# A hand-written order of all instructions, searched anew, in a 3x3 convolution with 2x2 max pooling

## Chip, cores and metric

One core of a Trainium2 chip runs the program. The metric is the device time of one execution in microseconds (us), the median of several runs.

## The reference

A 3x3 convolution with zero padding of one row and column, 16 images of 64 channels and 64x64 pixels, 128 output channels, and then the maximum over 2x2 squares:

```
x: (16, 64, 64, 64) float32, weight: (128, 64, 3, 3) float32, pool_size 2
x_pad = pad(x, 1)
conv[b, co, i, j] = sum over ci, kh, kw of weight[co, ci, kh, kw] * x_pad[b, ci, i + kh, j + kw]
output[b, c, i, j] = max(conv[b, c, 2i:2i+2, 2j:2j+2])          # (16, 128, 32, 32) float32
```

## The kernel before

Two images lie on the 128 partitions, 64 channels each, so a matmul uses one half of the rows of TensorE (PE) and two of them, one for each image, run side by side. A pair of images is cut into four chunks of 8 output rows; there are 32 chunks, numbered 0 to 31 in the order of their work. Eight are of the kind K (0, 2, 5, 9, 14, 18, 23, 27), the others of the kind W. A and B are the even and the odd convolution rows of a chunk. Rows are combined before the matmuls, so that A and B share products: a W chunk `s` and image `l` go through these steps, each named by a token.

- `LX.s` loads the rows into one of four buffers `wx` (SP's queue); `LK.s` loads a K chunk with a cast to bf16 (POOL's queue).
- `E.s`, `S.s` and `V.s` are sums and differences of rows (L195, or L289 where `CP.s`, an ACT copy of rows to PSUM, L285, gave one of the operands). `KS.s` is the sum of a K chunk. Tokens end in the engine: `v` is DVE, `a` is ACT, `g` is POOL. A row operation on POOL is made to wait for the last one on DVE ahead of it in the order (`row_op`, L194 to L199).
- `P2.s.l` starts A with `E`; `SE.s.l` copies it to B's PSUM bank (ACT, L422); `P0` and `P3` add `V` to A and to B; `EV` takes A to SBUF (ACT, L409 or L411); `MX` puts the maximum of A and B into B's bank (DVE, L426); `P1` adds `S`, which both have in common; `OD` copies the odd columns out (ACT, L449), `CM` takes the maximum with the even ones (DVE, L458), and `ST` stores the chunk.
- A K chunk has `PAa`, `PAb` for A, `PBa`, `PBb` for B and `PR` in place of `P1`; it reads its rows as they are, after `XE` and `XO` have cast them (even and odd rows) where they came as float32.

All products go through L394. Each has three matmuls of up to 512 columns, and two products that stand next to each other in the order, one for each image, are emitted alternately (`flush`). A number at the end of a product or of `SE` is its PSUM bank, one of eight; a bank is free again when its last reader is done.

The weights come in by `LW`. Seven combinations are made: `c.D2` and `c.D0` (differences of the kernel's rows, L205 and L207), `c.g0` to `c.g2` (casts), and `c.GS`, `c.GM`, `c.GP` (sums; GM and GP need GS). `T.x` transposes a combination on PE (L228), `TV.x` copies it back to SBUF (L239, L241, L243). `PAa` uses D2, `PAb` and `P0` G0, `PBa` D0, `PBb` and `P3` G2, `P2` GM, `PR` G1 and `P1` GP.

The order of everything is written out in one string, `ORDER`: a token is emitted when its turn comes, so each engine gets its own instructions in the order of the string, and semaphores follow from the data. Some loads also wait for the end of an earlier chunk (`paced`).

```
for token in ORDER.split():
    what, _, at = token.partition(":")
    name, *args = what.split(".")
    ...
```

Of the kernel before, what the change touches and what calls it, by code (L numbers as in the profile page):

```python
# [27 lines left out]
SE.6.1:5 MX.4.1 PR.2.0 PR.2.1 E.7:v P0.6.1 P1.4.0 SE.6.0:3 LX.12 OD.2.0 OD.2.1 EV.6.1 P3.6.1 P0.6.0
OD.4.0 EV.6.0 CM.2.0 P3.6.0 P1.4.1 CM.2.1 MX.6.1 CM.4.0 OD.4.1 PAa.5.1:6 P2.7.0:1 MX.6.0 CP.8:4
LX.15 PAa.9.0:0 P1.6.1 OD.6.1 CM.4.1 LX.16 CM.6.1 SE.7.0:2 P1.6.0 PAb.5.1 P2.7.1:7 PAb.9.0 ST.0  # L30
S.7:g PAa.9.1:5 P0.7.0 V.8:g E.8:v OD.6.0 E.10:g EV.5.1 EV.9.0 S.8:v CM.6.0 EV.7.0 KS.9:v PBa.5.1:6
P3.7.0 LK.14 PAb.9.1 PAa.5.0:4 ST.2 KS.5:v SE.7.1:0 CP.11:3 PBb.5.1 P2.8.0:1 V.10:g MX.7.0 E.11:v
LX.13 PAb.5.0 P0.7.1 MX.5.1 EV.9.1 P1.7.0 P3.7.1 S.11:v SE.8.0:5 E.12:v EV.7.1 P0.8.0 PR.5.1 EV.5.0
P2.10.1:7 PBa.5.0:3 OD.7.0 S.10:g MX.7.1 P2.8.1:4 P3.8.0 OD.5.1 CM.5.1 ST.4 V.12:g EV.8.0 P1.7.1
PBb.5.0 CM.7.0 SE.10.1:1 P0.10.1 P2.10.0:6 MX.8.0 MX.5.0 SE.8.1:2 OD.7.1 EV.10.1 CM.7.1 SE.10.0:0
P1.8.0 P3.10.1 ST.6 P0.8.1 PR.5.0 OD.8.0 P3.8.1 P2.12.0:7 MX.10.1 OD.5.0 P0.10.0 P1.10.1 CM.8.0
CM.5.0 EV.8.1 SE.12.0:5 P3.10.0 P2.11.1:4 MX.8.1 ST.1 LX.19 EV.10.0 P0.12.0 P1.8.1 SE.11.1:3 P3.12.0
PBa.9.1:6 V.11:g OD.8.1 OD.10.1 EV.12.0 LX.17 MX.10.0 LK.18 P1.10.0 P0.11.1 OD.10.0 S.12:v CM.8.1
CM.10.1 PBb.9.1 PAa.14.0:2 MX.12.0 EV.11.1 CM.10.0 P2.11.0:7 P3.11.1 ST.5 ST.3 CP.13:1 PAb.14.0
PAa.14.1:4 MX.9.1 SE.11.0:0 MX.11.1 EV.14.0 E.13:v P1.12.0 PR.9.1 OD.12.0 S.13:v P0.11.0 P1.11.1  # L40
OD.9.1 OD.11.1 CM.12.0 P2.13.1:2 P3.11.0 CM.11.1 EV.11.0 CM.9.1 MX.11.0 CP.17:5 SE.13.1:3 PBa.9.0:1
PAb.14.1 V.13:g PBb.9.0 P2.12.1:7 LX.22 S.16:g EV.14.1 E.16:g E.17:v SE.12.1:6 P1.11.0 P0.13.1
OD.11.0 EV.13.1 V.16:g P2.13.0:4 P3.13.1 MX.9.0 P0.12.1 PR.9.0 S.17:v SE.13.0:5 MX.13.1 P2.16.0:2
P3.12.1 EV.12.1 CM.11.0 E.15:g MX.12.1 OD.9.0 SE.16.0:7 P0.13.0 P1.13.1 OD.13.1 CM.9.0 LX.20 P3.13.0
P2.15.1:0 EV.13.0 V.15:g CM.13.1 MX.13.0 SE.15.1:1 P0.16.0 P1.12.1 ST.11 P2.15.0:3 PBa.14.1:4
KS.18:v P0.15.1 P3.16.0 ST.8 S.15:v KS.14:v OD.12.1 P1.13.0 PBb.14.1 CM.12.1 EV.16.0 SE.15.0:2
EV.15.1 P0.15.0 P3.15.1 LX.24 MX.14.1 PBa.14.0:6 P2.16.1:0 ST.10 MX.15.1 LX.21 P3.15.0 PR.14.1
EV.15.0 OD.13.0 SE.16.1:3 MX.16.0 PBb.14.0 P1.15.1 OD.14.1 CM.13.0 P2.17.1:5 P1.16.0 OD.15.1 LK.23
OD.16.0 MX.15.0 V.17:g CM.14.1 CM.15.1 P0.16.1 P1.15.0 SE.17.1:4 EV.16.1 P3.16.1 P2.17.0:1 MX.14.0
CM.16.0 V.20:g OD.15.0 MX.16.1 PR.14.0 P0.17.1 S.19:g SE.17.0:7 P3.17.1 PAa.18.0:0 CM.15.0 OD.14.0  # L50
P1.16.1 P0.17.0 CM.14.0 EV.17.1 CP.22:2 E.19:g MX.17.1 PAb.18.0 PAa.18.1:6 E.22:v OD.16.1 EV.17.0
P1.17.1 PBa.18.0:5 EV.18.0 CM.16.1 OD.17.1 S.22:v PAb.18.1 P2.19.0:1 CP.20:3 EV.18.1 CM.17.1
SE.19.0:2 PBa.18.1:0 P3.17.0 P2.19.1:4 PBb.18.0 V.19:g SE.19.1:6 PBb.18.1 P0.19.0 E.20:v S.20:v ST.7
MX.18.0 V.22:g P3.19.0 P0.19.1 MX.18.1 PR.18.0 P2.22.1:3 E.21:g EV.19.0 LX.26 MX.19.0 EV.19.1
PR.18.1 P2.20.0:1 OD.18.0 LX.28 MX.17.0 CM.18.0 V.21:g LX.25 SE.22.1:4 OD.18.1 CM.18.1 P3.19.1
P1.19.0 SE.20.0:5 P1.17.0 P0.22.1 OD.19.0 MX.19.1 P3.22.1 P2.21.0:0 EV.22.1 OD.17.0 CM.19.0 MX.22.1
P0.20.0 P1.19.1 P2.20.1:3 P3.20.0 SE.21.0:2 ST.9 OD.19.1 ST.13 KS.23:v CM.19.1 E.24:g EV.20.0
MX.20.0 P0.21.0 P1.22.1 P3.21.0 P2.21.1:1 LK.27 SE.20.1:6 P0.20.1 P1.20.0 CM.17.0 OD.22.1 CM.22.1
S.21:v EV.21.0 SE.21.1:7 EV.20.1 OD.20.0 V.24:g P3.20.1 P2.22.0:4 V.25:g E.26:g S.24:g MX.21.0
V.28:g P2.24.0:0 P0.21.1 SE.22.0:3 EV.21.1 MX.20.1 P1.21.0 P3.21.1 CM.20.0 OD.21.0 ST.18 SE.24.0:5  # L60
P0.22.0 P1.20.1 MX.21.1 P3.22.0 P2.24.1:1 EV.22.0 P1.21.1 P0.24.0 CM.21.0 LX.30 OD.20.1 SE.24.1:2
P3.24.0 PAa.23.1:4 ST.16 CM.20.1 EV.24.0 PAa.23.0:6 P0.24.1 MX.22.0 OD.21.1 P1.22.0 PAb.23.1 CM.21.1
CP.25:0 EV.24.1 E.25:v MX.24.0 PAb.23.0 PBa.23.1:7 EV.23.1 S.25:v OD.22.0 P2.25.0:1 P3.24.1 MX.24.1
EV.23.0 PBb.23.1 PBa.23.0:4 P2.25.1:6 P1.24.0 LX.29 ST.12 P1.24.1 PBb.23.0 SE.25.0:0 CM.22.0 OD.24.0
SE.25.1:3 MX.23.1 CM.24.0 MX.23.0 KS.27:v P0.25.0 PR.23.1 OD.24.1 EV.25.0 OD.23.1 P3.25.0 P0.25.1
PR.23.0 PAa.27.1:5 CM.24.1 V.26:g MX.25.0 EV.25.1 P2.26.1:1 PAa.27.0:2 ST.14 OD.23.0 ST.19 PAb.27.1
P1.25.0 CM.23.1 PAb.27.0 P3.25.1 CP.30:6 SE.26.1:7 CM.23.0 E.30:v S.30:v PBa.27.0:4 P3.26.1
P2.26.0:6 P0.26.1 EV.27.1 ST.20 OD.25.0 CP.28:5 MX.25.1 EV.27.0 E.28:v CM.25.0 PBb.27.0 P1.25.1
S.28:v S.26:g SE.26.0:2 MX.27.0 EV.26.1 ST.15 E.29:g PBa.27.1:0 P0.26.0 V.30:g MX.26.1 OD.25.1
P3.26.0 P2.28.1:1 EV.26.0 MX.26.0 PBb.27.1 PR.27.0 P1.26.1 P2.28.0:5 CM.25.1 SE.28.1:6 OD.27.0  # L70
V.29:g CM.27.0 ST.24 S.29:g MX.27.1 SE.28.0:3 OD.26.1 P1.26.0 P0.28.1 EV.28.1 P3.28.1 P2.29.0:4
P0.28.0 PR.27.1 OD.26.0 CM.26.1 SE.29.0:1 P2.29.1:7 P3.28.0 OD.27.1 EV.28.0 LX.31 ST.17 MX.28.1
P0.29.0 P1.28.1 CM.26.0 SE.29.1:2 ST.26 OD.28.1 MX.28.0 P3.29.0 P2.30.1:5 EV.29.0 CM.27.1 MX.29.0
SE.30.1:0 E.31:g P0.29.1 P1.28.0 EV.29.1 OD.28.0 P3.29.1 P2.30.0:4 CM.28.1 P1.29.0 P0.30.1 CM.28.0
SE.30.0:7 ST.27 EV.30.1 OD.29.0 MX.29.1 P3.30.1 P2.31.0:6 MX.30.1 ST.23 CM.29.0 ST.28 ST.22 V.31:g
# [509 lines left out]
```

## Time and profile before

| | |
|---|---|
| median of 3 runs | 105.04 us (104.89 to 105.57) |
| the profiled execution | 105.11 us |
| its span, first to last instruction | 103.3 us |
| granted clock of PE, mean | 0.987 |
| busy: PE, DVE, ACT, POOL | 96.6, 90.2, 88.8, 80.6 us |
| bytes moved by DMA | 24.07 MB, mean 233 GB/s |

The profile is of one execution. Busy times of the engines lie beside each other, so their sum says nothing; what counts is which of them is late at a given moment. PE is counted busy while any of its two halves has a matmul under way.

### The profile page before, as it was taken

Reading aid. Unit: us, or ns where it says so; the run is one execution under the profiler, and the core shown is the slowest. Engines: PE = TensorE matmul, PEld = TensorE weight load, DVE = VectorE, ACT = ScalarE, POOL = GpSimd, SP = SyncE. Lnnn points to the kernel's source line nnn. Section 1 sums busy time; section 2 is a strip of 40 time slices with the busy share of each in tenths; the row PEclk is TensorE's granted clock in tenths of the full one; section 3 lists DMA queues with packets and bytes.
Section 4 is the critical chain, followed back from the end, with each engine's and each line's share of the span. In section 5 each row is a group of like instructions: output and inputs, shape, how many; then the busy total and the mean of one; then the engine's idle time right before and its main releaser. Section 6 shows DMA issues by size and latency. Waiting matters only on the chain.

```text
span 103.3 us, 2470 instructions
## 1 busy us (share of the span) xinstructions
PE 96.6 (94%) x869; PEld 51.6 (50%) x869; DVE 90.2 (87%) x179; ACT 88.8 (86%) x198; POOL 80.6 (78%) x61
## 2 busy tenths in 40 slices
PE   6988699999999999999999999999999999999940
...
GB/s 65 260 251 414 420 421 352 303 115 179 36 274 247 215 360 290 309 253 185 205 115 246 309 195 177 360 307 275 186 356 205 142 231 40 0 133 285 337 187 83
DMA packets 13789, 24.07 MB, mean 233 GB/s; under 512 B 1104, under 2 KB 9680, under 8 KB 13776
## 3 DMA queue, kind: packets, MB, share of 16 engines
...
q0 software_dynamic: 864, 1.56, 10.1%
q8 instruction: 7, 0.11, 0.4%
q10 hardware_dynamic: 144, 0.07, 0.2%
...
## 4 chain that ended last, share of the span: by engine, by line
PE 80%; DMA 7%; DVE 4%; ACT 3%; SPq 1%; issue 1%; DVEq 0%
PE acc L394 80%; DMA wx<-in_x_dram 7%; ACT ev L409 1%; DVE o L458 1%; DVE acc L426 1%; ACT acc L422 1%; SPq L266 1%; ACT od L449 1%; DVE wv L195 1%; DVE we L195 0%; SPq L519 0%; DVEq L580 0%; DVE o L468 0%; DVEq L426 0%
## 5 line engine op out<-in xcount | busy, mean ns | idle before, releaser
L394 PEld LDWEIGHTS <-wt 64*128 64x128 bf16 x840 | 49.3, 94 | 42.8 <-issue 3.0
L195 POOL TENSOR_TENSOR wv<-wx 128x1024 bf16<-128x1024 f32 x23 | 54.1, 2363 | 12.9 <-DVE wv L195 9.3
L394 PE MATMUL acc<-wv,wt 64*128 64x504 bf16 (+1 forms) x288 | 61.1, 377 | 0.9 <-DVE acc L426 0.9
L426 DVE TENSOR_TENSOR acc<-acc,ev 128x512 f32<-128x512 f32 x64 | 43.4, 694 | 3.0 <-ACT ev L409 1.3
L394 PE MATMUL acc<-kx,wt 64*128 64x504 bf16 (+6 forms) x216 | 38.2, 350 | 0.2 <-DVE kx L190 0.2
L394 PE MATMUL acc<-we,wt 64*128 64x512 bf16 (+1 forms) x144 | 37.4, 377 | 0.3 <-DVE we L195 0.3
L394 PE MATMUL acc<-ws,wt 64*128 64x512 bf16 x144 | 37.5, 376 | 0.2 <-DVE acc L426 0.2
L409 ACT ACTIVATE ev<-acc 128x512 f32<-128x512 f32 x48 | 29.6, 616 | 1.8 <-PE acc L394 1.3
L422 ACT COPY acc<-acc 128x512 f32<-128x512 f32 x48 | 28.2, 593 | 1.2 <-PE acc L394 0.3
L458 DVE TENSOR_TENSOR o<-acc,od 128x256 f32<-128x256 f32 x63 | 25.4, 418 | 1.9 <-ACT od L449 1.6
L449 ACT COPY od<-acc 128x256 f32<-128x256 f32 x63 | 23.6, 383 | 2.8 <-PE acc L394 2.5
L195 POOL TENSOR_TENSOR ws<-wx 128x512 bf16<-128x512 f32 x9 | 11.5, 1273 | 1.4 <-DVE we L195 1.4
L394 PE MATMUL acc<-ks,wt 64*128 64x504 bf16 (+1 forms) x48 | 11.9, 376 | 0.0
L195 POOL TENSOR_TENSOR we<-wx 128x512 bf16<-128x512 f32 x9 | 11.5, 1275 | 0.4 <-DVE ks L195 0.4
L411 ACT COPY ev<-acc 128x512 f32<-128x512 f32 x16 | 9.4, 599 | 1.2 <-PE acc L394 1.2
L289 DVE TENSOR_TENSOR we<-acc,wx 128x512 bf16<-128x512 f32 x11 | 7.5, 686 | 0.2
L289 DVE TENSOR_TENSOR ws<-acc,wx 128x512 bf16<-128x512 f32 x11 | 7.5, 682 | 0.0
L285 ACT COPY acc<-wx 128x512 f32<-128x512 f32 x11 | 6.7, 610 | 0.8 <-DMA wx<-in_x_dram 0.8
L486 PE MATMUL acc<-const-bfloat16-1.0 128*128 128x512 bf16 x8 | 3.6, 628 | 0.8 <-PEq L566 0.8
L270 POOL DMA_DIRECT2D kx<-in_x_dram x6 | 3.5, 592 | 0.0
L195 DVE TENSOR_TENSOR ks<-kx 128x512 bf16<-128x512 bf16 x8 | 3.4, 438 | 0.0
L195 DVE TENSOR_TENSOR we<-wx 128x512 bf16<-128x512 f32 x4 | 2.7, 684 | 0.7 <-DMA wx<-in_x_dram 0.7
...
## 6 DMA issues: line engine op xcount, KB each, us to landing
...
```

The source lines that it names most:

```text
L195: inst = eng[e].tensor_tensor(out=out, in0=in0, in1=in1, op=op)
L270: paced(s, nc.gpsimd.dma_start(out=kx_of(p)[:, lo:hi, :], in_=rows_of(p, lo, hi)))
L285: nc.scalar.copy(out=acc[bank], in_=wrow(s, 0))
L289: nc.vector.tensor_tensor(out=t, in0=lifted[s], in1=wrow(s, 1), op=op)
L394: yield lambda kw=kw, o0=o0, o1=o1, c0=c0, c1=c1: nc.tensor.matmul(acc[t][:, i0:i1, o0:o1], wt[l * CI : l * CI + CI, K * BLOCKS[block] + T ...
L409: inst = nc.scalar.mul(t, acc[bank["A", s, l]], -1.0)
L411: inst = nc.scalar.copy(out=t, in_=acc[bank["A", s, l]])
L422: nc.scalar.copy(out=acc[b], in_=acc[bank["A", s, l]])
L426: nc.vector.tensor_tensor(out=t, in0=t, in1=ev[s, l], op=MAX)
L449: nc.scalar.copy(out=od[s, l][:, i0:i1], in_=acc[bank["B", s, l]][:, i0:i1, 1::2])
L458: done[s, l] = nc.vector.tensor_tensor(out=outs(s)[:, l, i0:i1], in0=acc[bank["B", s, l]][:, i0:i1, 0::2], in1=od[s, l][:, i0:i1], op=MAX,)
L486: nc.tensor.matmul(acc[n], ones[:, 0:128], ones, start=True, stop=True, skip_group_check=True)
```

## The change

Only `ORDER` is another; the helpers, the tiles and the number of buffers are the same. Both strings hold the same 287 products and transposes and the same 62 issues on SP's queue. These tokens change engine:

| token | before | after |
|---|---|---|
| c.g1 | ACT | DVE |
| c.GS | DVE | POOL |
| TV.D0, TV.G0 | ACT | DVE |
| TV.G2, TV.GM | DVE | ACT |
| XE.0b, XO.0b | DVE | ACT |
| V.4 | POOL | DVE |
| E.4, E.7 | DVE | POOL |
| E.10, E.16 | POOL | DVE |
| S.12, S.21 | DVE | POOL |

Banks and places change throughout. The diff, cut to the head, the places that the text speaks of, and the end:

```
-LW LX.0a c.g0:a LX.0b c.g1:a c.g2:a XE.0a:a c.D0:v T.D0:0 LX.1 XO.0a:a c.D2:v LX.3 T.D2:1 T.G0:2
-LX.2 c.GS:v c.GM:v T.G2:3 T.G1:4 TV.D2:v TV.D0:a XE.0b:v T.GM:5 TV.G0:a LX.4 XO.0b:v PAa.0.0a:6
-PAa.0.1a:7 PBa.0.0a:1 PBa.0.1a:0 TV.G2:v PAa.0.1b PAb.0.0a c.GP:v TV.G1:a TV.GM:v KS.0:v E.1:v
-PAa.0.0b PAb.0.1a PAb.0.1b PAb.0.0b PBa.0.0b PBa.0.1b EV.0.1 EV.0.0 LX.7 PBb.0.1a PBb.0.0a T.GP:2
-TV.GP:a PBb.0.1b PBb.0.0b P2.1.0:3 P2.1.1:4 CP.3:5 V.1:v LX.6 MX.0.1 SE.1.0:7 P0.1.0 PR.0.1 SE.1.1:6
-V.3:g MX.0.0 P0.1.1 PR.0.0 XO.2:a E.3:v EV.1.0 LK.5 OD.0.1 S.3:v EV.1.1 S.1:v PAa.2.0:2 P3.1.1
-XE.2:a CM.0.1 S.4:g MX.1.1 P2.3.0:3 PAa.2.1:5 OD.0.0 P2.3.1:4 PAb.2.0 CM.0.0 KS.2:v E.4:v LK.9 V.4:g
-SE.3.0:0 P1.1.1 P3.1.0 EV.2.0 MX.1.0 SE.3.1:1 OD.1.1 CP.6:2 PAb.2.1 P3.3.0 P0.3.1 P0.3.0 V.6:g LX.11
...
+LW c.D2:v c.D0:v T.D2:0 c.g0:a LX.0a XO.0a:a XE.0a:a LX.0b c.g2:a c.g1:v LX.1 LX.3 TV.D2:v T.D0:1
+T.G0:2 TV.D0:v PAa.0.0a:3 PAa.0.1a:4 LX.2 T.G2:5 PBa.0.0a:6 PBa.0.1a:7 XE.0b:a T.G1:0 c.GS:g TV.G0:v
+XO.0b:a LX.4 TV.G1:a c.GM:v T.GM:1 PAb.0.1a PBa.0.0b LX.7 LX.6 c.GP:v T.GP:2 KS.0:v TV.G2:a PAb.0.0a
+PAa.0.1b PBb.0.0a E.1:v PAa.0.0b PAb.0.1b PBb.0.0b PBb.0.1a TV.GM:a PBa.0.1b PAb.0.0b PBb.0.1b
+EV.0.1 TV.GP:a V.1:v EV.0.0 MX.0.1 P2.1.0:0 P2.1.1:5 CP.3:1 SE.1.0:4 PR.0.1 P0.1.0 E.3:v SE.1.1:3
+XO.2:a EV.1.0 P2.3.1:2 P3.1.0 S.3:v P0.1.1 PAa.2.0:1 V.3:g MX.0.0 S.1:v V.4:v SE.3.1:0 XE.2:a EV.1.1
+LK.5 PR.0.0 P0.3.1 OD.0.0 LX.10 LX.8 OD.0.1 MX.1.0 LK.9 S.4:g E.4:g P3.3.1 PAb.2.0 E.7:g CM.0.0
+EV.3.1 EV.2.0 P2.3.0:5 P3.1.1 MX.1.1 SE.3.0:2 PAa.2.1:6 P1.1.0 V.6:g CM.0.1 OD.1.0 MX.3.1 P1.1.1
+P0.3.0 CP.6:1 CM.1.0 PBa.2.0:7 PAb.2.1 OD.1.1 EV.3.0 E.6:v EV.2.1 P2.4.1:4 P3.3.0 P1.3.1 P2.4.0:5
...
+P2.6.0:0 OD.3.0 KS.2:v P0.4.0 P3.4.1 EV.4.1 V.7:g CM.3.0 SE.6.0:2 MX.2.1 LX.11 MX.4.1 P2.6.1:4
+P3.4.0 EV.4.0 PR.2.1 P0.6.0 SE.6.1:5 MX.4.0 EV.6.0 E.10:v LK.14 P1.4.1 PR.2.0 LX.12 P3.6.0 P0.6.1
...
+OD.4.0 V.10:g SE.7.0:1 CM.2.0 CM.4.0 PAa.5.0:4 PBa.5.1:7 P2.7.1:3 P0.7.0 KS.5:v EV.5.1 S.7:g OD.6.0
...
+LX.13 SE.10.1:4 EV.9.1 SE.10.0:2 P1.8.0 P0.10.1 PBb.5.0 P3.10.1 KS.9:v KS.14:v SE.8.1:5 P0.10.0
+P0.8.1 EV.10.1 E.12:v OD.8.0 S.12:g EV.10.0 P2.11.1:6 P3.10.0 MX.5.0 P3.8.1 PR.5.0 CM.8.0 MX.10.1
+MX.10.0 P2.12.0:3 P1.10.1 EV.8.1 SE.11.1:0 V.12:g LX.16 OD.5.0 P0.11.1 P1.10.0 CM.5.0 OD.10.1 MX.8.1
+SE.12.0:7 EV.11.1 PAa.14.0:1 P3.11.1 ST.2 OD.10.0 E.16:v ST.1 P0.12.0 P1.8.1 OD.8.1 EV.12.0 MX.11.1
...
+CM.13.1 EV.13.0 LX.20 CP.17:1 MX.13.0 P1.12.1 P0.16.0 EV.16.0 E.17:v ST.7 PBa.14.1:5 P3.16.0
+SE.15.1:2 ST.6 S.17:v OD.12.1 CM.12.1 PBb.14.1 P2.15.0:6 SE.15.0:1 ST.11 ST.10 P1.13.0 P0.15.1
...
+PBa.18.1:3 CM.15.0 MX.17.1 PBa.18.0:1 PAb.18.1 E.19:g EV.17.0 ST.8 CM.16.1 CP.22:2 LX.25 P2.19.0:4
...
-P2.31.1:3 P0.30.0 SE.31.0:5 EV.30.0 S.31:g P3.30.0 P1.29.1 MX.30.0 SE.31.1:1 P0.31.0 P1.30.1 OD.29.1
-CM.29.1 EV.31.0 OD.30.1 P3.31.0 P0.31.1 EV.31.1 P1.30.0 P3.31.1 MX.31.0 P1.31.0 OD.30.0 MX.31.1
-CM.30.1 P1.31.1 ST.25 ST.21 ST.29 OD.31.0 ST.30.1 CM.30.0 ST.30.0 CM.31.0 ST.31.0 RM.31.1a RM.31.1b
-ST.31.1a ST.31.1b:a
+MX.30.1 SE.31.0:2 P2.31.1:5 P0.30.0 EV.30.0 P3.30.0 P1.29.1 CM.29.0 MX.30.0 SE.31.1:4 OD.29.1
+P0.31.0 P1.30.1 CM.29.1 ST.28 EV.31.0 P3.31.0 P0.31.1 EV.31.1 MX.31.0 S.31:g P1.30.0 P3.31.1 P1.31.0
+ST.24 MX.31.1 ST.29 OD.30.0 CM.30.0 OD.30.1 CM.30.1 ST.30.0 OD.31.0 ST.30.1 CM.31.0 P1.31.1 ST.31.0
+RM.31.1a RM.31.1b ST.31.1a ST.31.1b:a
```

More of the change, by code (lines that the diff above doesn't have):

```diff
@@ L22 @@
-V.3:g MX.0.0 P0.1.1 PR.0.0 XO.2:a E.3:v EV.1.0 LK.5 OD.0.1 S.3:v EV.1.1 S.1:v PAa.2.0:2 P3.1.1
-XE.2:a CM.0.1 S.4:g MX.1.1 P2.3.0:3 PAa.2.1:5 OD.0.0 P2.3.1:4 PAb.2.0 CM.0.0 KS.2:v E.4:v LK.9 V.4:g
-SE.3.0:0 P1.1.1 P3.1.0 EV.2.0 MX.1.0 SE.3.1:1 OD.1.1 CP.6:2 PAb.2.1 P3.3.0 P0.3.1 P0.3.0 V.6:g LX.11
-CM.1.1 P3.3.1 P1.1.0 E.6:v EV.3.1 EV.2.1 PBa.2.0:6 PBa.2.1:4 EV.3.0 MX.3.1 P2.4.0:5 P1.3.1 OD.1.0
-OD.3.1 S.6:v LX.10 PBb.2.0 P2.4.1:3 MX.3.0 PBb.2.1 P1.3.0 CM.1.0 SE.4.0:2 SE.4.1:7 CM.3.1 OD.3.0
-MX.2.0 V.7:g P2.6.1:1 P0.4.0 CM.3.0 P0.4.1 P3.4.0 EV.4.0 MX.2.1 LX.8 MX.4.0 EV.4.1 P2.6.0:0 P3.4.1
@@ L28 @@
[L28 to L75, printed above, removed]
@@ new lines @@
+P0.3.0 CP.6:1 CM.1.0 PBa.2.0:7 PAb.2.1 OD.1.1 EV.3.0 E.6:v EV.2.1 P2.4.1:4 P3.3.0 P1.3.1 P2.4.0:5
+S.6:v MX.3.0 CM.1.1 SE.4.1:6 OD.3.1 PBb.2.0 PBa.2.1:1 CM.3.1 SE.4.0:3 P1.3.0 P0.4.1 MX.2.0 PBb.2.1
+P2.6.0:0 OD.3.0 KS.2:v P0.4.0 P3.4.1 EV.4.1 V.7:g CM.3.0 SE.6.0:2 MX.2.1 LX.11 MX.4.1 P2.6.1:4
+P3.4.0 EV.4.0 PR.2.1 P0.6.0 SE.6.1:5 MX.4.0 EV.6.0 E.10:v LK.14 P1.4.1 PR.2.0 LX.12 P3.6.0 P0.6.1
+PAa.5.1:0 P1.4.0 OD.4.1 CM.4.1 OD.2.1 EV.6.1 MX.6.0 P3.6.1 P2.7.0:6 PAb.5.1 P1.6.0 CM.2.1 OD.2.0
+OD.4.0 V.10:g SE.7.0:1 CM.2.0 CM.4.0 PAa.5.0:4 PBa.5.1:7 P2.7.1:3 P0.7.0 KS.5:v EV.5.1 S.7:g OD.6.0
@@ new lines @@
+V.8:g MX.6.1 ST.0 PBb.5.1 PAb.5.0 CM.6.0 CP.8:0 EV.7.0 S.10:g V.11:g ST.3 P3.7.0 P1.6.1 SE.7.1:2
+E.8:v MX.5.1 S.8:v P0.7.1 PAa.9.0:6 MX.7.0 EV.5.0 OD.6.1 LX.15 EV.7.1 CM.6.1 P3.7.1 P2.8.0:4 CP.11:0
+PR.5.1 PAb.9.0 SE.8.0:3 EV.9.0 MX.7.1 P1.7.0 PAa.9.1:5 E.11:v P1.7.1 P0.8.0 S.11:v OD.7.0 OD.5.1
+P3.8.0 P2.10.1:6 CM.7.0 PAb.9.1 P2.10.0:0 CM.5.1 P2.8.1:1 PBa.5.0:7 EV.8.0 MX.8.0 OD.7.1 CM.7.1
+LX.13 SE.10.1:4 EV.9.1 SE.10.0:2 P1.8.0 P0.10.1 PBb.5.0 P3.10.1 KS.9:v KS.14:v SE.8.1:5 P0.10.0
+P0.8.1 EV.10.1 E.12:v OD.8.0 S.12:g EV.10.0 P2.11.1:6 P3.10.0 MX.5.0 P3.8.1 PR.5.0 CM.8.0 MX.10.1
```

34 lines of the change are left out of this document (added).

## The prediction

> **What bounds the kernel now.** I read the page first: which engine is full, and where it is not.
>
> ```profile
> span 103.3 us, 2470 instructions
> PE 96.6 (94%) x869; PEld 51.6 (50%) x869; DVE 90.2 (87%) x179; ACT 88.8 (86%) x198; POOL 80.6 (78%) x61
> PE   6988699999999999999999999999999999999940
> ```
>
> PE is full from the fifth slice to the 38th. What a new order can win lies ahead of that stretch, behind it, or in small losses inside it. The chain of waits gives its start:
>
> ```profile
> 2.10 7.21 DMA wx<-in_x_dram
> ...
> 11.80 33.61 PE acc L394 x302
> ```
>
> The chain comes from the first W load, LX.1, landing at 9.31. From there I read the timeline of DVE, one row or merged group at a time, and of the other engines around it:
>
> ```profile
> 9.34 0.69 DVE L195 TENSOR_TENSOR we<-wx 128x512 bf16<-128x512 f32 x1 [0.66 <-DMA wx<-in_x_dram]
> 9.95 1.22 DVE L195 TENSOR_TENSOR wv<-wx 128x1024 bf16<-128x1024 f32 x1
> 11.08 1.29 DVE L426 TENSOR_TENSOR acc<-acc,ev 128x512 f32<-128x512 f32 x2
> 12.28 0.68 DVE L289 TENSOR_TENSOR we<-acc,wx 128x512 bf16<-128x512 f32 x1
> 12.88 0.68 DVE L289 TENSOR_TENSOR ws<-acc,wx 128x512 bf16<-128x512 f32 x1
> 13.48 0.69 DVE L195 TENSOR_TENSOR ws<-wx 128x512 bf16<-128x512 f32 x1
> 14.42 0.68 DVE L426 TENSOR_TENSOR acc<-acc,ev 128x512 f32<-128x512 f32 x1
> 15.02 0.41 DVE L458 TENSOR_TENSOR o<-acc,od 128x256 f32<-128x256 f32 x1
> 15.35 0.55 DVE L195 TENSOR_TENSOR ks<-kx 128x512 bf16<-128x512 bf16 x1
> ...
> 10.08 0.82 PE L394 MATMUL acc<-we,wt 64*128 64x512 bf16 x6 [0.30 <-DVE we L195]
> 10.67 0.59 ACT L285 COPY acc<-wx 128x512 f32<-128x512 f32 x1 [0.77 <-DMA wx<-in_x_dram]
> 11.20 1.04 ACT L422 COPY acc<-acc 128x512 f32<-128x512 f32 x2
> 11.25 2.37 POOL L195 TENSOR_TENSOR wv<-wx 128x1024 bf16<-128x1024 f32 x1 [9.28 <-DVE wv L195]
> ```
>
> These are E.1, V.1, then MX.0.1 and MX.0.0, E.3, S.3, S.1 on DVE; P2.1, CP.3, SE.1 and V.3 elsewhere. PR.0.1 cannot start before MX.0.1 ends, near 11.78. So 9.31 + E.1 + V.1 + MX.0.1 sets 11.80. DVE starts an instruction 0.60 after a 0.68 one (12.28 to 12.88) and 0.33 after a 0.41 one (15.02 to 15.35); I walk its queue with these steps.
>
> Now the dense stretch. Every pair of products (six matmuls, three on each half of the rows) takes one step:
>
> ```profile
> 23.33 0.39 PE L394 MATMUL acc<-wv,wt 64*128 64x512 bf16 x1
> ...
> 94.73 0.38 PE L394 MATMUL acc<-ws,wt 64*128 64x512 bf16 x1
> ...
> 95.38 0.38 PE L394 MATMUL acc<-ws,wt 64*128 64x512 bf16 x1
> ```
>
> One pair goes from 94.73 to 95.38: 0.645 by the finer starts. The row at 95.38 is the pair P0.31.0 and P1.30.1. By the order string it is the 127th pair after P0.1.0, in the old order and in the new. 11.80 + 127 x 0.645 = 93.72, so the old order loses 1.66 us inside the dense stretch. The row at 23.33 is the 17th pair: 11.80 + 17 x 0.645 = 22.77, so 0.56 is lost by then and 1.10 later. This 1.66 is all that the middle can give back. Behind 95.38 come 7.92 us of tail.
>
> **The change part by part.** The durations I use, from the groups by line and from the timeline of the head:
>
> ```profile
> L195 POOL TENSOR_TENSOR wv<-wx 128x1024 bf16<-128x1024 f32 x23 | 54.1, 2363 | 12.9 <-DVE wv L195 9.3 <-DVE ks L195 1.8 <-DVE ws L195 1.3
> L195 POOL TENSOR_TENSOR ws<-wx 128x512 bf16<-128x512 f32 x9 | 11.5, 1273 | 1.4 <-DVE we L195 1.4
> L409 ACT ACTIVATE ev<-acc 128x512 f32<-128x512 f32 x48 | 29.6, 616 | 1.8 <-PE acc L394 1.3
> L422 ACT COPY acc<-acc 128x512 f32<-128x512 f32 x48 | 28.2, 593 | 1.2 <-PE acc L394 0.3 <-DVE ws L289 0.2
> L449 ACT COPY od<-acc 128x256 f32<-128x256 f32 x63 | 23.6, 383 | 2.8 <-PE acc L394 2.5
> L195 DVE TENSOR_TENSOR gsum<-wraw 128x192 f32<-128x192 f32 x1 | 0.5, 507 | 0.0
> ...
> 3.72 0.61 DVE L207 TENSOR_TENSOR wq<-wraw 128x256 bf16<-128x256 f32 x1 [2.59 <-DMA wraw<-in_weight_dram]
> 6.79 0.49 DVE L190 CAST kx<-kf 128x256 bf16<-128x256 f32 x2 [0.57 <-DMA kf<-in_x_dram]
> 5.38 0.78 ACT L188 CAST kx<-kf 128x320 bf16<-128x320 f32 x2
> 6.05 1.23 ACT L239 COPY wt<-acc 128x384 bf16<-128x384 bf16 x3
> 5.86 0.35 DVE L243 COPY wt<-acc 128x384 bf16<-128x384 bf16 x1
> 6.28 0.83 PE L394 MATMUL acc<-kx,wt 64*128 64x256 bf16 x12
> 7.34 1.74 PE L394 MATMUL acc<-kx,wt 64*128 64x256 bf16 x30 [0.23 <-DVE kx L190]
> ```
>
> **Head: 0.** D2 now comes ahead of D0, and TV.D2, TV.D0 and TV.G0 run on DVE. g1 moves to DVE; its cost there is not shown and lies between a cast of that size, 0.25 (half of 0.49), and the strided sum, 0.51. I take the upper, which it is nearer to, since both read the weights with a stride. TV.D2 then ends near 5.6 and the first product starts there instead of at 6.28: 0.6 earlier. It buys nothing. P2.1 still waits for E.1, hence for LX.1, and the first nine issues on SP's queue are the same in both orders, so 9.31 stays. The 0.6 turns into a wait ahead of 10.08.
>
> Does the work of chunk 0 still fit ahead of 10.08? The casts XE.0b and XO.0b move to ACT, which gets them at 6.79 and needs 0.8 for both (5.38 row); TV.G1 and TV.G2 add 0.8 (1.23 for three), to about 8.35. Behind TV.G2 stand five steps of half-size products, 0.35 each (1.74 for thirty matmuls, six a step): 10.1, just in time. GS moves from DVE to POOL, where nothing of its shape is seen. Below it costs what DVE takes, 0.51; above, a whole POOL row operation, 1.27. GM needs it only near 6.1, and LW has landed by 3.7 (the row at 3.72): hidden at both ends, behind DVE's six head operations. Without that cover it would cost its whole duration.
>
> **First 17 pairs: +0.1.** V.4 moves from POOL (2.36) to DVE (1.22), behind S.1. DVE's queue becomes E.3 11.68, S.3 12.28, MX.0.0 12.88, S.1 13.48, V.4 14.08, MX.1.0 15.2, CM.0.0 15.8, ending at 16.2. Behind CM.0.0 waits PAa.2.1: it writes bank 6, which holds chunk 0's result until CM.0.0 has read it. It is the seventh pair, due at 11.80 + 6 x 0.645 = 15.67, and starts near 16.25. Also SE.3.1 and SE.3.0 have two steps, 1.29, between P2.3 and P0.3, while a product takes 0.82 and SE 0.59: 0.1 to 0.2 each, partly inside the same delay. I find 0.64 lost by the 17th pair against 0.56. Ends: no loss if V.4's 1.14 step fell into idle time of DVE, and the whole 1.14. DVE has no gap here, so the value lies between; E.4, behind S.4 on POOL, is ready at 17.9 for P2.4.1 at 18.2.
>
> **Other exchanges: 0 by themselves.** E.4 and E.7 go to POOL, E.10 and E.16 to DVE; S.12 and S.21 go to POOL. POOL's sum is -2.36 + 2 x 1.27 = +0.2, DVE's 1.22 - 2 x 0.68 = -0.1. Stores and loads are issued in another sequence on SP's queue, the same number; each load lands well ahead of its first reader, and an output buffer is written again no sooner than 5 us after its store is free to go. ACT's sums don't change.
>
> **Pairs 17 to 127: 0, in two parts.** Row operations on DVE that read two SBUF tiles and those on POOL take turns in this trace:
>
> ```profile
> 14.32 1.28 POOL L195 TENSOR_TENSOR ws<-wx 128x512 bf16<-128x512 f32 x1
> L195 DVE TENSOR_TENSOR ks<-kx x8: 410/416/545, 8.3 to 79.8; 128x512 bf16<-128x512 bf16 x8
> 16.58 7.01 POOL L195 TENSOR_TENSOR wv<-wx 128x1024 bf16<-128x1024 f32 x3 [0.48 <-DVE we L195]
> 23.50 0.68 DVE L195 TENSOR_TENSOR we<-wx 128x512 bf16<-128x512 f32 x1
> ```
>
> E.7 begins at 23.50, as V.7 ends at 23.59; KS.2, which came at 15.35 with S.4 running to 15.60, took 0.55 where the least is 0.41. The Trainium skill (GPSIMD Engine Reference, "8. Key points") says that GPSIMD shares its SBUF interfaces with VectorE and contends with DVE instructions that have two SBUF inputs; the trace agrees, by 0.13 on KS.2. It gives no price.
>
> Walking POOL's new queue with 2.32 and 1.24 a step, KS.2 finds POOL busy for 0.3 more, E.10 for 0.45, KS.5 for 0.55 and KS.9 for 0.5. KS.9, KS.14 and E.12 then end at 36.2, S.12 and V.12 behind them (POOL's row operations wait for the last one on DVE) at 39.9, and P0.12.0 was due at 39.5: 0.4 late. MX.10.1 runs 0.2 late in the same place, mostly inside that 0.4. Later I find P2.15.0, which needs EV.16.0's bank two steps after P0.16.0 (0.82 + 0.62 against 1.29: 0.2) and E.19 (0.15 late for P2.19.0). Together 0.8. The old order has 1.10 there, of which I leave 0.3 as small losses that have no place; with the same 0.3 the new one loses 1.1. Ends: 0.3 if the hand-overs hide in idle time, 2.1 if each of those four waits (1.8) reaches PE beside the 0.3.
>
> **Tail: 0.** The last five groups of products are the same. EV.31.1 now comes ahead of one OD of 0.38, but MX.31.1 waits for MX.31.0 anyway; the two follow each other on DVE without a gap:
>
> ```profile
> 96.95 1.38 DVE L426 TENSOR_TENSOR acc<-acc,ev 128x512 f32<-128x512 f32 x2 [0.17 <-PE acc L394]
> ```
>
> Sum: 0 + 0.1 + 0 + 0 = +0.1 on the profiled execution, whose own time is 105.11 (span 103.3 and 1.8 around it): 105.2. That execution is 0.07 above the median shown, 105.04.
>
> **The rivals.**
> - Slower: DVE and POOL get out of turn. POOL is the queue with the least slack (78% busy over the span, nearly without gaps after 16.58), and every POOL operation put behind a DVE row operation inherits its delay. If the waits of 0.3, 0.45, 0.55 and 0.5 all arrive at PE, beside 0.64, 0.35 for P2.15.0 and E.19, 0.3 and the 0.2 of MX.10.1, the dense stretch loses 3.3 instead of 1.66: 106.7. It decides once P0.12.0 starts more than 1 us late. Against it: DVE has 13% idle time that can swallow part.
> - The head ends later: ACT has 10.1 against 10.08. If its casts of strided rows take 0.15 more each, P2.1 slips by 0.3 and SE.1.0 with it; 105.5.
> - Faster: nothing is lost behind the 17th pair but the 0.3, and V.4 on DVE costs half. Then the stretch loses 0.6 instead of 1.66: 104.0. For it: only three places in the new middle have a dependence two steps long or a late row operation. Against it: PE pairs still run in step with DVE at 87% and ACT at 86%.
> - The reordering of D2 and D0 does not do what it says: it starts the first product earlier and the end of the head stays. That is how the forecast has it, and it has no chance of its own.
>
> **How the numbers follow.** Chances: forecast 105.2, 0.40; late head 105.5, 0.13; DVE and POOL out of turn 106.7, 0.30; little lost 104.0 or less, 0.17. A measurement of this kernel tells about 1%, 1.05 us, from no change. The first two lie within it, 0.53; the third is slower, 0.30; the fourth I count as faster, 0.17. The range: from the fast case, 104.0, to the slow one, 106.7. The forecast's own range is 104.5 to 105.9.
>
> **What would show it.** Right: the first matmul on kx near 5.6, P2.1 still at 10.08 and the chain's PE part from 11.80; a second wv row of 1.22 on DVE near 14.1, the seventh pair near 16.25; POOL with 22 wv and 11 ws; the pair P0.31.0 near 95.5. Wrong: the dense part starting elsewhere than 11.7 to 12.1; P0.12.0 on time, which frees 0.4; P0.31.0 below 94.5 or above 96.4.

## The result, and the profile after

The new order is slower by 1.4%. Its median is 106.77 us (15 runs, 105.55 to 107.31), that of the order before, beside it on the same chips, 105.13 us (15 runs). The ratio is 1.0143, with a 95% interval of 1.0108 to 1.0177; ratios here and below leave disturbed runs out. On the 105.04 that the forecast started from, the ratio makes 106.5. The forecast was 105.2, its range ended at 106.7.

The page of the new kernel, with the rows that answer to those of before:

```profile
span 105.0 us, 2477 instructions
PE 98.6 (94%) x869; PEld 57.4 (55%) x869; DVE 90.5 (86%) x176; ACT 89.5 (85%) x199; POOL 82.0 (78%) x63
PE   7799799999999999999999999999999999999950
L195 POOL TENSOR_TENSOR wv<-wx 128x1024 bf16<-128x1024 f32 x22 | 51.8, 2366 | 8.1 <-DVE wv L195 6.7
L195 POOL TENSOR_TENSOR ws<-wx 128x512 bf16<-128x512 f32 x11 | 14.0, 1276 | 3.7 <-DVE ks L195 2.0
```

The engines are about as busy as before and POOL has the 22 and 11 operations that were expected of it. PE's row is the reading: the slices with 9 look alike, and PE is no emptier in the head (slices 1 to 5) than it was. That is misleading. A matmul at half speed counts as busy, and PE has more busy time here (98.6 against 96.6) for the same 869 matmuls.

The chain of waits of the new kernel (start, us, what):

```profile
0.74 2.79 DMA wraw<-in_weight_dram
...
3.55 0.61 DVE wq L205
4.17 1.17 DVE wq L207
...
5.38 0.82 PE acc L228 x6
...
9.71 1.03 PE acc L394 x12
...
10.76 0.59 ACT ev L411
...
11.63 0.45 ACT ev L411
...
12.09 0.06 ACT acc L285
...
12.61 0.60 ACT acc L422
...
13.25 4.26 PE acc L394 x35
```

The head is another one. Before, the chain ran from the landing of LX.1 over E.1, V.1 and MX.0.1. Now it runs from the weights over D0 (L207), the transposes and all products of chunk 0 on PE, and then EV.0.1, EV.0.0, CP.3 and SE.1.0 on ACT. The dense stretch (P0.1.0) begins at 13.25, not at 11.80: 1.45 later.

From there on little differs. Rows of the timeline of PE, new kernel:

```profile
13.25 0.37 PE L394 MATMUL acc<-wv,wt 64*128 64x512 bf16 x1 [0.56 <-ACT acc L422]
...
24.89 0.38 PE L394 MATMUL acc<-ks,wt 64*128 64x512 bf16 x1
...
97.21 0.38 PE L394 MATMUL acc<-ws,wt 64*128 64x512 bf16 x1
```

These are P0.1.0, the later product of the 17th pair (the other starts 0.12 before it) and the 127th pair, with P0.31.0. From P0.1.0 to P0.31.0 it takes 83.96 (before: 95.38 - 11.80 = 83.58), behind it 105.0 - 97.2 = 7.8 (before 7.9). So +1.45 in the head, +0.38 in the middle, -0.1 in the tail: 1.7, which is the difference of the spans. Of the 1.45, 0.29 is the landing of LX.1, 9.60 in this execution instead of 9.31; 1.16 is lost behind it.

The rows that explain the head, from the timelines of the four engines:

```profile
3.55 0.61 DVE L205 TENSOR_TENSOR wq<-wraw 128x256 bf16<-128x256 f32 x1 [2.42 <-DMA wraw<-in_weight_dram]
4.08 1.25 DVE L207 TENSOR_TENSOR wq<-wraw 128x256 bf16<-128x256 f32 x1
3.60 1.25 POOL L195 TENSOR_TENSOR gsum<-wraw 128x192 f32<-128x192 f32 x1 [1.64 <-DMA wraw<-in_weight_dram]
4.22 0.50 PE L228 MATMUL acc<-ident,wq 128*128 128x128 bf16 x3
5.38 0.82 PE L228 MATMUL acc<-ident,wq 128*128 128x128 bf16 x6 [0.66 <-DVE wq L207]
6.14 0.82 PE L394 MATMUL acc<-kx,wt 64*128 64x256 bf16 x6
9.37 0.34 PE L228 MATMUL acc<-ident,wq 128*128 128x128 bf16 x3
9.64 1.82 PE L394 MATMUL acc<-kx,wt 64*128 64x192 bf16 x30
8.26 0.71 ACT L188 CAST kx<-kf 128x256 bf16<-128x256 f32 x2 [2.33 <-DMA kf<-in_x_dram]
8.88 0.85 ACT L239 COPY wt<-acc 128x384 bf16<-128x384 bf16 x2
9.62 0.50 ACT L239 ACTIVATE wt<-acc 128x384 bf16<-128x384 bf16 x1
```

Three things are to be seen. GS on POOL (3.60 to 4.85) lies beside D0 on DVE, which takes 1.25 where D2 just ahead of it took 0.61. T.D0 waits for D0, and PE idles 0.66 ahead of 5.38. The transposes and products behind that run at half speed (three transposes 0.50, at 9.37 again 0.34). And ACT waits 2.33 for the load LX.0b (8.23) before it casts XE.0b and XO.0b (8.26); TV.G1, TV.G2 and TV.GM queue behind these until 10.12. Two paths meet here. PE runs without a gap from 5.38 to the end of chunk 0 at 11.46, so T.D0 and the half speed alone would make it this late. But PBa.0.0b, the first product that reads a row of these casts, starts at 8.83, and XE.0b is done only at 8.66: the load alone would make it nearly as late.

The speed by the groups of PE between 4 and 9 us, first before, then after:

```profile
L394 PE MATMUL acc<-kx,wt 64*128 64x252 bf16 x24 | 2.3, 269 | 0.0
```

```profile
L394 PE MATMUL acc<-kx,wt 64*128 64x252 bf16 x8 | 1.3, 416 | 0.0
```

The same matmul takes 416 ns on the mean instead of 269. The trace's record of the full granted clock begins at 9.08 in this execution, and at 4.98 in the one of before.

### The profile page after: what moved, and what is told of

Same layout as the page of the kernel before. It is cut to its first block, busy times and chain, and to the rows that moved or that the text cites. A ratio compares the mean times of both kernels' runs of the same rounds, so it can differ in the third digit from the quotient of the medians.

```text
span 105.0 us, 2477 instructions
## 1 busy us (share of the span) xinstructions
PE 98.6 (94%) x869; PEld 57.4 (55%) x869; DVE 90.5 (86%) x176; ACT 89.5 (85%) x199; POOL 82.0 (78%) x63
## 4 chain that ended last, share of the span: by engine, by line
PE 86%; DVE 4%; DMA 3%; ACT 2%; issue 1%; DVEq 0%
PE acc L394 84%; DMA wraw<-in_weight_dram 3%; PE acc L228 2%; DVE acc L426 1%; DVE wq L207 1%; DVE o L458 1%; ACT ev L411 1%; DVE wq L205 1%; ACT acc L422 1%; DVE o L468 0%; DVEq L580 0%; ACT wt L239 0%; ACT acc L285 0%; DVEq L458 0%
## 5 line engine op out<-in xcount | busy, mean ns | idle before, releaser
L394 PEld LDWEIGHTS <-wt 64*128 64x128 bf16 x840 | 54.6, 95 | 38.0 <-issue 4.8
L394 PE MATMUL acc<-wv,wt 64*128 64x504 bf16 (+1 forms) x288 | 64.1, 377 | 0.6 <-ACT acc L422 0.6
L195 POOL TENSOR_TENSOR wv<-wx 128x1024 bf16<-128x1024 f32 x22 | 51.8, 2366 | 8.1 <-DVE wv L195 6.7
L394 PE MATMUL acc<-kx,wt 64*128 64x504 bf16 (+7 forms) x216 | 38.7, 359 | 0.0
L394 PE MATMUL acc<-ws,wt 64*128 64x512 bf16 (+1 forms) x144 | 37.1, 376 | 0.2
L449 ACT COPY od<-acc 128x256 f32<-128x256 f32 x63 | 23.1, 385 | 1.4 <-PE acc L394 1.1
L195 POOL TENSOR_TENSOR ws<-wx 128x512 bf16<-128x512 f32 x11 | 14.0, 1276 | 3.7 <-DVE ks L195 2.0
L394 PE MATMUL acc<-ks,wt 64*128 64x504 bf16 (+1 forms) x48 | 12.9, 377 | 0.2 <-DVE acc L426 0.2
L411 ACT COPY ev<-acc 128x512 f32<-128x512 f32 x16 | 9.5, 594 | 0.8 <-PE acc L394 0.8
L188 ACT CAST kx<-kf 128x256 bf16<-128x256 f32 (+2 forms) x6 | 2.8, 490 | 2.7 <-DMA kf<-in_x_dram 2.7
```

Source lines behind the costliest of these rows:

```text
L195: inst = eng[e].tensor_tensor(out=out, in0=in0, in1=in1, op=op)
L394: yield lambda kw=kw, o0=o0, o1=o1, c0=c0, c1=c1: nc.tensor.matmul(acc[t][:, i0:i1, o0:o1], wt[l * CI : l * CI + CI, K * BLOCKS[block] + T ...
L411: inst = nc.scalar.copy(out=t, in_=acc[bank["A", s, l]])
L449: nc.scalar.copy(out=od[s, l][:, i0:i1], in_=acc[bank["B", s, l]][:, i0:i1, 1::2])
```

## The experiments

Tokens are those of the head, engine letter behind the colon. Each run is compared with the order before, run beside it on the same chip.

**The two kernels again, unaltered.** One profiled execution each.

> The changed kernel unaltered, profiled a second time. Its first profile has LX.0b landing at 8.23 us (one of sixteen parts late, the others by 6.15) and the full TensorE clock from 9.08 us, against 6.77 and 4.98 in the kernel before. Theory clock: GS on POOL holds D0 on DVE (1.25 us instead of 0.61), PE stands for 0.66 us between T.D2 and T.D0, and the clock comes late in some executions, depending on where the gap falls; D0 again takes 1.2 us or so, in every execution. Theory landing: the late part of LX.0b alone made the head late; then a profile with LX.0b by 7 us has the pair P0.1.0 near 11.8. Theory body: neither, P0.1.0 may start at 11.8 and the time is still about 106.5.

107.25 us; P0.1.0 at 13.65, LX.0b at 8.63, D0 1.23, full clock from 9.62, 83.98 from P0.1.0 to P0.31.0. The late head is no accident of one execution.

> The kernel before, unaltered, profiled a second time. In its first profile LX.0b landed at 6.77 us; in the five others so far, all with the same first nine issues, at 7.42 to 8.63. If the landing simply scatters, it is likely near 7.5 here and P0.1.0 still starts near 12.0, because in this order the weight copies on ACT do not stand behind XE.0b. If the landing depends on the order, it is near 6.8 again.

105.43 us; P0.1.0 at 12.23 with LX.1 landing at 9.74 instead of 9.31: 2.49 behind the landing both times. LX.0b lands at 7.36 here instead of 6.77 and costs nothing.

**The old head in front of the new middle and tail.**

```
-LW c.D2:v c.D0:v T.D2:0 ... EV.0.1 TV.GP:a V.1:v EV.0.0 MX.0.1
+LW LX.0a c.g0:a LX.0b c.g1:a ... PBb.0.1b PBb.0.0b V.1:v MX.0.1    # head of before, other banks
 P2.1.0:0 P2.1.1:5 CP.3:1 SE.1.0:4 PR.0.1 P0.1.0 E.3:v ...           # as after
```

> The head of the order before (all tokens up to P2.1, its banks renumbered to those that the rest needs), then the new order from P2.1 on. If all of the loss lies in the head, 105.0 to 105.2. If the loss is in the middle (DVE and POOL out of turn, V.4 on DVE), it stays: 106.3 to 106.7. My prediction's walk of the middle says +0.1 for this kernel: 105.2.

105.15 us, ratio 0.9981 (0.9945 to 1.0016). The whole loss is in the head. P0.1.0 starts at 12.06, 2.52 behind LX.1; the stretch to P0.31.0 takes 83.79, 0.2 more than before.

**GS back on DVE.**

```
-... T.G1:0 c.GS:g TV.G0:v
+... T.G1:0 c.GS:v TV.G0:v
```

> GS back on DVE at its place in the new order, one token's engine changed. Theory clock: D0 takes 0.61, T.D0 starts near 4.9, the clock is full by 5 to 8 us, and most of the head's loss goes: 105.3 to 105.8. Theory landing: no more than 0.2 us gained, since XE.0b still waits: 106.4 to 106.8. Theory body: the same, 106.4 to 106.8.

105.86 us, ratio 1.0060 (1.0023 to 1.0098): 0.8 of the 1.4% is gone, with one letter. That is just above what theory clock gave, and below the 106.4 of the two others. Its timelines:

```profile
4.24 0.61 DVE L207 TENSOR_TENSOR wq<-wraw 128x256 bf16<-128x256 f32 x1
5.59 0.50 DVE L195 TENSOR_TENSOR gsum<-wraw 128x192 f32<-128x192 f32 x1
7.50 0.71 ACT L188 CAST kx<-kf 128x256 bf16<-128x256 f32 x2 [1.22 <-DMA kf<-in_x_dram]
10.77 0.59 ACT L411 COPY ev<-acc 128x512 f32<-128x512 f32 x1
11.23 0.62 ACT L285 COPY acc<-wx 128x512 f32<-128x512 f32 x1
11.75 1.09 ACT L422 COPY acc<-acc 128x512 f32<-128x512 f32 x2
```

D0 takes 0.61 as soon as nothing runs on POOL beside it. The sum itself costs DVE 0.50 instead of POOL 1.25. EV.0.0, CP.3 and SE.1.0 still follow each other on ACT without a gap, so the other part of the loss stays.

**The gap on PE filled.** GS stays on POOL and D0 stays held; two matmuls on constants, which nobody reads, stand behind T.D2.

```
-LW c.D2:v c.D0:v T.D2:0 c.g0:a ...
+LW c.D2:v c.D0:v T.D2:0 WU.512:6 WU.256:7 c.g0:a ...
```

> GS stays on POOL; two filler matmuls (512 and 256 columns of ones, into banks that later products clear) stand between T.D2 and T.D0, so that PE has no gap there. D0 is still held. Theory clock: the clock is full by 5 to 8 us, the products of chunk 0 take half the time, 105.4 to 106.0. Theory landing and theory body: 106.4 to 106.9.

106.29 us, ratio 1.0098 (1.0060 to 1.0135), between the two forecasts. The rows of PE's timeline:

```profile
4.62 0.80 PE L526 MATMUL acc<-const-bfloat16-1.0 128*128 128x512 bf16 x2
5.47 0.51 PE L228 MATMUL acc<-ident,wq 128*128 128x128 bf16 x6
6.04 0.50 PE L394 MATMUL acc<-kx,wt 64*128 64x256 bf16 x6
```

T.D0 starts no earlier (5.47), yet the six transposes take 0.51 instead of 0.82 and the first product 0.50 instead of 0.82; the full clock is granted from 5.25. In this trace the clock comes early where the gap is filled. In the times, about half of what GS costs would thus be the late clock, but that is not shown: the interval overlaps that of the new kernel (1.0108 to 1.0177) and that of GS on DVE.

**The two casts behind TV.G1 and TV.G2 on ACT**, so that ACT need not wait for the load; then the same with GS on DVE.

```
-... PBa.0.1a:7 XE.0b:a T.G1:0 c.GS:g TV.G0:v XO.0b:a LX.4 TV.G1:a c.GM:v ... KS.0:v TV.G2:a PAb.0.0a
+... PBa.0.1a:7 T.G1:0 c.GS:g TV.G0:v TV.G1:a TV.G2:a XE.0b:a XO.0b:a LX.4 c.GM:v ... KS.0:v PAb.0.0a
```

> The changed kernel with GS on POOL as it is, but XE.0b and XO.0b moved on ACT behind TV.G1 and TV.G2, so that ACT does not stand still for LX.0b with weight copies queued behind. Theory queue on ACT (head loss from LX.0b's landing through ACT's queue): 0.4 to 0.8 us gained, 106.0 to 106.3. Theory GS and clock alone: 106.5 to 106.8, since T.D0 is late and the products of chunk 0 run at half clock all the same.

> GS on DVE and XE.0b, XO.0b behind TV.G1 and TV.G2 on ACT. If these two account for the head, P0.1.0 starts at 11.8 to 12.1 and the time is 104.9 to 105.3, that of the kernel before. If something else of the new head costs, it stays at 105.6 to 105.9 as with GS alone.

106.88 us, ratio 1.0145 (1.0124 to 1.0166), and 106.09 us, ratio 1.0094 (1.0078 to 1.0110). The expected gain did not come; the second is no better than GS on DVE alone (1.0060, the intervals overlap). ACT and PE in the first:

```profile
7.86 0.86 ACT L239 COPY wt<-acc 128x384 bf16<-128x384 bf16 x2 [1.89 <-DVE wq L195]
8.61 0.72 ACT L188 CAST kx<-kf 128x256 bf16<-128x256 f32 x2
9.07 0.48 PE L394 MATMUL acc<-kx,wt 64*128 64x256 bf16 x5 [0.90 <-ACT kx L188]
```

LX.0b had landed at 6.36, and ACT stood idle for 1.89 all the same, now for TV.G1, ahead of which the weights and T.G1 (done at 7.82) have to be ready. The casts began at 8.61, later than behind the load, and PE waited 0.90 for them. So the wait for the load was not the whole of it: what counts is when XE.0b and XO.0b are done, whatever ACT waits for in front of them. They are done at 8.97 in the new kernel and 9.33 here; chunk 0 ends 2.3 to 2.5 later in both, and 2.25 to 2.72 later in all fourteen profiles.

In these two runs the full clock came early in the profiles, at 4.44 and 4.96, so they show what the held D0 does by itself. It moves TV.G1 from 7.26 to 7.86, the casts from 8.00 to 8.61 and P0.1.0 from 12.78 to 13.38: where ACT passes it on, the hold costs its 0.6 without any late clock.

**The two casts back on DVE, with GS on POOL and on DVE.**

```
-... XE.0b:a T.G1:0 c.GS:g TV.G0:v XO.0b:a LX.4 TV.G1:a c.GM:v T.GM:1 ...
+... T.G1:0 c.GS:g TV.G0:v LX.4 TV.G1:a c.GM:v T.GM:1 c.GP:v XE.0b:v XO.0b:v ...    # or c.GS:v
```

> The same with GS left on POOL: D0 is held, T.D0 comes at 5.4, the rest of the head follows 0.6 later. Theory of two causes: half of the loss stays, 105.6 to 106.2. Rival, that GS on POOL only matters through the queue of ACT: 104.9 to 105.3.

> The changed kernel with GS on DVE and the casts XE.0b and XO.0b on DVE too, behind GP. Theory of two causes (GS on POOL holds D0; the casts on ACT put LX.0b's landing and 0.8 us of casts ahead of the weight copies and of EV.0.1, TV.GP, EV.0.0, CP.3 and SE.1.0, which ACT does one after another): both gone, SE.1.0 ends near 11.9 and the time is 104.8 to 105.3. Rival, that the new order of the products of chunk 0 is itself the second cause: 105.5 to 105.9, as with GS alone on DVE.

105.58 us, ratio 1.0064 (1.0023 to 1.0105), and 105.50 us, ratio 1.0009 (0.9990 to 1.0028). The 105.50 touches what the rival gave, but the order before took 105.34 on this chip, and the ratio leaves no loss. Three tokens, with two of them put behind GP, undo the whole loss. Each of the two moves, put back alone, was worth about 0.8%, both together 1.3%: they overlap.

The 1.0064 is a mean of two kinds of executions. Of the runs that it is taken from, eight took 105.47 to 105.71 us, as long as the kernel with both moved back (105.24 to 105.63, all twelve), and three took 106.62 to 106.97. The profile is of one of the eight: D0 is held there (1.23), PE has its gap, and the full clock came ahead of the gap, at 4.35. So with the casts on DVE the hold alone costs almost nothing, and GS costs 1.1 to 1.4 in some executions only. That the clock came late in these is likely, but none of them was traced. A late LX.0b would do the same, but it would have had to spare all twelve runs with both moves back.

The kernel with both moved back:

```profile
7.41 0.49 DVE L190 CAST kx<-kf 128x256 bf16<-128x256 f32 x2
11.28 0.69 DVE L426 TENSOR_TENSOR acc<-acc,ev 128x512 f32<-128x512 f32 x1
5.62 0.51 PE L394 MATMUL acc<-kx,wt 64*128 64x256 bf16 x6
8.45 1.81 PE L394 MATMUL acc<-kx,wt 64*128 64x192 bf16 x30
12.06 0.37 PE L394 MATMUL acc<-wv,wt 64*128 64x512 bf16 x1
10.43 0.59 ACT L411 COPY ev<-acc 128x512 f32<-128x512 f32 x1
10.89 0.62 ACT L285 COPY acc<-wx 128x512 f32<-128x512 f32 x1
11.41 1.08 ACT L422 COPY acc<-acc 128x512 f32<-128x512 f32 x2
```

The casts are done at 7.90, chunk 0 at 10.26, and the end of SE.1.0 on ACT (12.01) and that of MX.0.1 on DVE (11.97) come together: the dense stretch starts 2.55 behind LX.1 (9.51), as in the order before. LX.0b landed at 6.71 in this execution, so the casts waited for DVE and not for the load.

**Each of the two moves alone in the order before, and the exchange of D2 and D0 alone.**

```
-LX.2 c.GS:v ...          -... XE.0b:v ... XO.0b:v         -... c.D0:v T.D0:0 LX.1 XO.0a:a c.D2:v LX.3 T.D2:1
+LX.2 c.GS:g ...          +... XE.0b:a ... XO.0b:a         +... c.D2:v T.D2:1 LX.1 XO.0a:a c.D0:v LX.3 T.D0:0
```

> The kernel before with GS on POOL, one token's engine: the suspect alone in the old head. D2 (here the second) is held for 0.6 us, so TV.D2 and the first products come 0.6 later, but the products of chunk 0 wait for LX.0b near 7.4 anyway. Two causes: 105.2 to 105.6. If it costs what it cost in the new order: 105.9 to 106.1.

> The kernel before with XE.0b and XO.0b on ACT at their places: TV.G0, TV.G1 wait behind them for LX.0b. Two causes: 0.4 to 1.0 us slower, 105.6 to 106.2. If the casts on ACT do not matter: 105.1 to 105.3.

> The kernel before with D2 and D0 exchanged (and their transposes), nothing else: the first part of the change alone. My prediction gave it nothing: 105.0 to 105.3. A rival: the first products start earlier, PE has less idle time and the clock comes sooner: 104.5 to 104.9.

105.00 us, ratio 0.9992 (0.9962 to 1.0023); 105.32 us, ratio 1.0000 (0.9968 to 1.0032), where a loss of 0.4 to 1.0 was expected and missed; 105.19 us, ratio 0.9995 (0.9973 to 1.0018). None costs or brings anything beyond its interval. The first, with GS on POOL, came out below both of its forecasts:

```profile
3.72 1.25 POOL L195 TENSOR_TENSOR gsum<-wraw 128x192 f32<-128x192 f32 x1 [1.76 <-DMA wraw<-in_weight_dram]
4.20 1.24 DVE L205 TENSOR_TENSOR wq<-wraw 128x256 bf16<-128x256 f32 x1
8.22 1.07 ACT L411 COPY ev<-acc 128x512 f32<-128x512 f32 x2 [0.99 <-PE acc L394]
```

The second, with the casts on ACT:

```profile
6.99 0.41 ACT L188 CAST kx<-kf 128x256 bf16<-128x256 f32 x1 [0.26 <-DMA kf<-in_x_dram]
7.67 0.41 ACT L188 CAST kx<-kf 128x256 bf16<-128x256 f32 x1
9.23 1.07 ACT L411 COPY ev<-acc 128x512 f32<-128x512 f32 x2 [0.77 <-PE acc L394]
11.11 0.59 ACT L285 COPY acc<-wx 128x512 f32<-128x512 f32 x1 [0.41 <-DMA wx<-in_x_dram]
```

The second operation on DVE is held here too (D2 now, 1.24), and the casts run on ACT here too. But in the old order both EVs of chunk 0 (the row of two at L411) are done by 9.3 and 10.3, while CP.3 starts only at 10.7 and 11.1, when LX.3 has landed, and SE.1.0 behind it. The old order finishes `PAa` and `PAb`, which make A, first and computes `PBb` under the two EVs; the new one has `PBa.0.1b PAb.0.0b PBb.0.1b` last and then EV.0.1, TV.GP and EV.0.0 in one line ahead of CP.3. In the six profiles with the old head ACT stands idle for 0.2 to 1.3 ahead of CP.3, and SE.1.0 ends with MX.0.1 or before it. In the eight with the new head ACT has no idle time there, and SE.1.0 ends last. So the old head had slack on this path, the new one none. That the place of EV.0.0 took it is read from these timelines; no run moved EV.0.0 alone, and none made both moves in the old order.

The head in numbers (us from the start of the span, one profiled execution each):

| | ratio | LX.0b | LX.1 | D0 | EV.0.0 ends | P0.1.0 | behind LX.1 |
|---|---|---|---|---|---|---|---|
| before | 1 | 6.77 | 9.31 | 0.61 | 9.51 | 11.80 | 2.49 |
| after | 1.0143 | 8.23 | 9.60 | 1.25 | 12.22 | 13.25 | 3.65 |
| GS on DVE | 1.0060 | 7.48 | 9.01 | 0.61 | 11.36 | 12.40 | 3.39 |
| casts on DVE | 1.0064 | 5.83 | 9.37 | 1.23 | 11.18 | 12.22 | 2.85 |
| both on DVE | 1.0009 | 6.71 | 9.51 | 0.60 | 11.03 | 12.06 | 2.55 |
| casts late | 1.0145 | 6.36 | 9.27 | 1.24 | 12.34 | 13.38 | 4.11 |
| casts late, GS on DVE | 1.0094 | 6.09 | 9.49 | 0.61 | 11.74 | 12.78 | 3.29 |
| old head, new middle | 0.9981 | 7.55 | 9.54 | 0.62 | 10.30 | 12.06 | 2.52 |

The column of LX.0b shows why a single profile can't be set against a ratio to a tenth: the landing alone moves by 2.4 between executions. It was 7.42 to 8.63 in the four profiles from one chip and 5.83 to 7.36 in the eight from two others, so parts that were measured on different chips add up only roughly. No version is faster than the order before by more than its interval.

## Why the prediction was right or wrong

**Head: 0. This step failed;** it was +1.45, 1.16 of it behind the landing of LX.1. Three of its terms did.

- "GS ... hidden at both ends, behind DVE's six head operations." Its duration was inside the bounds (1.25, bounds 0.51 and 1.27), and it ended at 4.85, in time for GM. What was not hidden is what it does to its neighbour: D0 on DVE went from 0.61 to 1.25, and T.D0, the first products and the clock with it. The prediction had the rule at hand. It used the take-turns of DVE and POOL, and the Trainium skill's sentence on shared SBUF interfaces (GPSIMD Engine Reference, "8. Key points"), for four places in the middle, and not for the one place in the head where a POOL operation and two DVE operations with two SBUF inputs are released by the same load. The price seen there had been 0.13; here it is 0.63. Both are what was left of POOL's operation when DVE's began (15.35 to 15.60 and 4.08 to 4.85), less 0.12 and 0.14.
- "ACT, which gets them at 6.79 ... 10.1, just in time." The sizes were right: the casts took 0.71 (0.8 forecast), TV.G1 and TV.G2 0.85 (0.8). But the term was walked with one landing of LX.0b, from one execution. It lands between 5.83 and 8.63 in the fourteen profiles. On DVE the order before lived with 7.36 at no cost; in the new order ACT's queue hands a delay on to TV.G1, TV.G2 and TV.GM, and the products of chunk 0 wait for the casts.
- "9.31 + E.1 + V.1 + MX.0.1 sets 11.80" was kept as the bound of the new order. It holds only while EV.0.0 is done long before CP.3. In the new order ACT's EV.0.0, behind the last products, then CP.3 and SE.1.0 are the bound; ACT was walked up to the end of chunk 0's products and no further.

The first product was to start near 5.6. It started at 6.14 with D0 held and at 5.62 in the run with both moves undone: that part of the walk was right but for D0.

**D2 and D0 in the order of use buy nothing:** right, 0.9995 alone.

**First 17 pairs: +0.1; the rest of the middle: 0.** Right. With a head that ends on time, the seventh pair starts at 16.51 behind P0.1.0 at 12.06 (old head, new middle), 0.58 behind its step of 0.645 (predicted 0.58), the two products of the 17th have lost 0.61 and 0.72 (predicted 0.64), and P0.31.0 has lost 1.88 against 1.66: +0.2. Of the single waits that were listed, P0.12.0 was on time, while P2.15.0 and P2.19.0 were 0.2 to 0.3 late: the hand-overs of DVE and POOL in the middle hid in idle time. In the new kernel itself the middle loses another 0.2, most of it at P2.25.0: it starts at 77.65, when E.25 (76.90, 0.69) is done. With the old head this pair has no delay; why E.25 comes later relative to PE stays open.

**Tail: 0.** Right (7.8 against 7.9).

**The rivals.** DVE and POOL out of turn in the middle gave 106.7, close to what was measured, for a place where little of it happened; the old head with the new middle rules it out. That the 106.5 lies inside the range is luck for this reason: the slow end was worked out for another mechanism. "The head ends later" had the place and one of its two causes, and was too small: 0.3 where the casts on ACT and GS on POOL cost 1.3% together. Its chance, 0.13, was too low for a margin of 0.02 us that rested on one landing.

**What stays open.** How often the clock comes late, and that it is what makes some executions slow. There are five profiles with an operation on DVE held and the gap on PE left open. In three of them the full clock was granted at 3.67, 4.35 and 4.44, ahead of the gap; in the two of the new kernel it was not yet granted when the gap began, and came at 9.08 and 9.62. So few profiles give no frequency, and the 0.8% of GS is not split into the late D0 and the late clock: with the casts on DVE the first was near nothing, with the casts late on ACT it was 0.6 us.
